# Moving the largest expert and the last pair of small ones in the order of 32 experts, with its row turning and one eviction placed elsewhere

## The chip, the core and the metric

One core of a Trainium2 chip runs the whole kernel. TensorE (PE in the profile) multiplies into PSUM; VectorE (DVE), ScalarE (ACT) and GpSimd (POOL) work beside it; SyncE (SP) issues the weight loads. All work in order, each on its own queue, and wait for one another by semaphores. The metric is the device time of one execution, in microseconds (us).

## The reference

A hybrid encoder layer on 512 tokens of width 1024: RMSNorm, one input projection into four head groups (stick-breaking attention, RG-LRU, HGRN2, Mamba-2), an output projection with a residual, and then a mixture of experts (MoE), which is where the change lies:

```python
logits = (xt @ router_w + router_b); top_logits, top_idx = lax.top_k(logits, 4)   # 32 experts
gates = softmax(top_logits)
# for each expert e, over the tokens routed to it:
hmid = xt[tok] @ w_gu[e] + b_gu[e]                  # 1024 -> 2048
glu = minimum(hmid[:, 0::2], 7); lin = clip(hmid[:, 1::2], -7, 7)
act = glu * sigmoid(1.702 * glu) * (lin + 1)
y = act @ w_down[e] + b_down[e]                     # 1024 -> 1024
# per token: the sum over its 4 experts of gate * y, added to h; a final RMSNorm
```

All of it is float32. Every expert has 12 MB of weights (8 MB for the first product, 4 MB for the second), and each is read once.

## The kernel before

The part ahead of the MoE is not touched. The router sorts the experts by their number of tokens, and the table CAPS gives each rank a capacity in rows: the largest 160, twelve others 120 to 72, sixteen 64, one 32, two 64. The experts are then worked one after another in an order written out by hand: the string SEQ (L55) names the kind of each place, and BIG says at which H, counted from 0, the largest expert stands. Rank r of a kind goes to the next place of that kind.

**Three kinds of expert.** H ("large", 65 to 128 rows) multiplies in a fast float32 mode that needs each operand in two parts, so each weight chunk is split on the fly: ACT copies it to the high part (L613) and DVE subtracts to get the low part (L614), in half chunks of 128x1024 through three buffers, so at most three half chunks ahead of PE. Three products of two matmuls each use one half chunk (L629). L ("small", 64 rows) and B (32 rows) multiply the chunk as it is, in plain float32, two (four) matmuls side by side in PE's columns (L658 and L729; L724 for B's second product). The largest expert is an H of 128 rows and a B of 32 rows in the same place; they share its weights.

**A stage.** The loop over the order (`for j, us in enumerate(seq)`) has one pass, here called stage j, per expert. In stage j, PE does: the bias of expert j (L644); its first product, in 8 steps k, one weight chunk each; then, while DVE and ACT do the activation of j (`act`, L674 to L679), the second product of expert j-1 in 8 steps f, two per chunk. At the end `yout(prev)` brings the result of j-1 out of PSUM with its gates (ACT L742 or L761, DVE L744 or L763), and `back` transposes the activation of j for its second product (L696; L687 for a B). So a stage that holds an H after an L is 8 chunks of fast product and 4 of plain product, and an L after an H the other way round.

**What is threaded between the steps.** `prepare` fetches the rows of a later expert: `onehot` (DVE L549), then `ids` (four small matmuls L556 into a PSUM bank, and the DVE reduction L557 that empties it) and a gather by POOL. `turn` transposes fetched rows into the layout for the first product (PE L585, then ACT L589 or L593, DVE L597 or L591). Rows are fetched and turned in groups: one per H, and one for up to 128 rows of L and B in a row. The dictionary `where` says in which stage a group is turned: "A" in the first product of an H, at k == 2; "B" at f == 5 of the second product of an H; "M" right after `act`. A "M" group of a stage with two units used the second half of the PSUM tile `hL` and one bank of the two-bank pool `m`. That tile's first half holds the first product of the B unit. `hot` (DVE L770) makes the matrix S which puts an expert's rows back to their tokens, and `add` (PE L789, DVE L791) adds all finished experts to the output in the stage after an H.

**Loads.** Weight chunks of 1 MB are loaded by SP in exactly the order of use, into a ring of 11 buffers: 8 chunks of expert j, then 4 of j-1's second product. A buffer is free when PE (for L, B) or the split on DVE (for H) has read it. The loads can so run less than one expert ahead of PE.

Stage numbers before, with the kinds: 0 L, 1 L, 2 H, 3 L, 4 H, 5 L, 6 L, 7 H+B (the largest), 8 L, 9 H, 10 L, 11 L, 12 H, 13 L, 14 H, 15 L, 16 L, 17 H, 18 L, 19 H, 20 L, 21 L, 22 H, 23 L, 24 H, 25 L, 26 H, 27 L, 28 H, 29 B, 30 H, 31 L. In stage 0, `run(first, ...)` threads the steps of the router's tables between the matmuls, one step after each k, and from k == 4 on one more in the middle.

Of the kernel before, what the change touches and what calls it, by code (L numbers as in the profile page):

```python
# [51 lines left out]

CAPS = (160, 120, 104, 104, 96, 96, 88, 80, 80, 72, 72, 72, 72) + 16 * (64,) + (32, 64, 64)

SEQ, BIG = "LL" + 4 * "HLHLL" + 3 * "HL" + "HBHL", 2  # L55
NSP = 3
FIN = "aaqqrAQrASQrAQrSSss"

# [420 lines left out]
def moe(ctx, tc, a, out, acc, c, loads, rt, mp, mp_es, hp, s2p, bp, early, once_es):  # L479
# [6 lines left out]
    def bank():  # L486
        return ps["m"].tile([128, 512], F32, name="m")
# [32 lines left out]
    N = len(seq)  # L520
# [125 lines left out]
    def gemm1(us, chunk, k, splits, limit, mid=lambda: None):  # L646

        W = chunk(k)
        last = k == KD - 1
        for u in us:  # L650
            if u.kind == "H":
                for half in range(2):
                    wh, wl = splits.take()
                    three(u.h[2 * half:2 * half + 2], u.xH[:, k, :], u.xL[:, k, :], wh, wl, False, last)
                    splits.make(limit)
            else:
                for q in range(4):
                    nc.tensor.matmul(u.h[q], u.xT[:, k, :], W[:, 512 * q:512 * q + 512], start=False, stop=last)  # L658
                    if q == 1:
                        mid()  # L660
# [20 lines left out]
    def back(us):  # L681

        for u in us:
            if u.kind == "B":
                p = u.views[0][1]
                for j in range(2):
                    nc.tensor.transpose(p[:, 128 * j:128 * j + 128], u.av[:, j:256:2], ident)  # L687
                u.aT = s2p.tile([128, 512], F32, tag="s2", name="aT")[:, 0:256].rearrange("p (j q n) -> p j q n", j=2, q=4)
                nc.scalar.activation(u.aT.rearrange("p j q n -> p (j q n)"), p[:, 0:256], AF.Copy)
                continue  # L690
            ps_ = [u.bk[0][:, 0:512], u.bk[1][:, 0:512]] if u.kind == "H" else [u.views[0][1][:, 0:512]]
            m = u.m
            for b, p in enumerate(ps_):
                for t_ in range(4):
                    f0 = 512 * b + 256 * (t_ // 2) + t_ % 2
                    nc.tensor.transpose(p[:, m * t_:m * t_ + m], u.av[0:m, f0:512 * b + 256 * (t_ // 2) + 256:2], ident[0:m, 0:m])  # L696
            if u.kind == "H":
                aH = wk.tile([128, KD, 128], FR, name="aH")
                aL = wk.tile([128, KD, 128], FR, name="aL")
                u.aH, u.aL = aH[:, :, 0:m], aL[:, :, 0:m]  # L700
                pv = [p[:, 0:4 * m].rearrange("p (k n) -> p k n", n=m) for p in ps_]
                for b in range(2):
                    nc.scalar.activation(u.aH[:, 4 * b:4 * b + 4, :], pv[b], AF.Copy)
                for b in range(2):
                    nc.vector.tensor_tensor(u.aL[:, 4 * b:4 * b + 4, :], pv[b], u.aH[:, 4 * b:4 * b + 4, :].bitcast(F32), op=OP.subtract)
            else:
                u.aT = wk.tile([128, 4, 2, 64], F32, name="aTL")
                nc.scalar.activation(u.aT.rearrange("p k g n -> p (k g n)"), ps_[0], AF.Copy)
# [56 lines left out]
    def hot(us):  # L765

        for u in us:
            if u.S is None:
                u.S = wk.tile([128, T], FR, name="S", bufs=3)[0:u.m]
                nc.vector.tensor_scalar(u.S, iota[0:u.m, :], u.tok[0:u.m, :], None, op0=OP.is_equal)  # L770
# [22 lines left out]
    splits = Splits([loads.of(j) for j, us in enumerate(seq) if us[0].kind == "H"])  # L793
# [3 lines left out]
    for g, us in enumerate(groups):  # L797
        j = us[0][0].j
# [21 lines left out]
    def turn_at(x, j, banks):  # L820
        for g in where.get((x, j), []):
            while g not in have:
                prepare()
            turn(g, *have[g], banks())
            turned.add(g)

    two = lambda: [bank(), bank()]
    halves2 = lambda: (lambda h: [h[:, 0:512], h[:, 512:1024]])(pair())
# [5 lines left out]
    def run(g, n=1000):  # L834
        for _ in range(n):
            if next(g, "end") == "end":
                return
# [5 lines left out]
    first = steps(rt.tables(), rt.more())  # L843
# [6 lines left out]
            ids(seq[e][0])  # L850
            yield

    pending = []
    for j, us in enumerate(seq):
        u = us[0]
        kind = u.kind
        if j == 1:
            once_es.close()
            sp = splits.pool = ctx.enter_context(tc.tile_pool(name="sp", bufs=NSP))
        if j == 2:  # L860
            mp_es.close()
            hL = ctx.enter_context(tc.tile_pool(name="hL", bufs=1, space=PSUM, side="right"))
            ps["m"] = ctx.enter_context(tc.tile_pool(name="m2", bufs=2, space=PSUM, side="right"))
        if j >= 1:
            loads.before(j + 1)

        if j == 0:
            u.views, u.h = [(0, rt.h0[0])], rt.h0[1]
        else:
            hL_ = [pair() if j < 2 else hL.tile([128, 1024], F32, name="hL")] if us[-1].kind != "H" else None  # L870
            light = lambda: hL_
            for x in us:
                if x.kind == "H":
                    x.bk = [pair(), pair()]
                bias(x, x.bk if x.kind == "H" else light() if x.kind == "L" else [light()[0][:, 0:512]])
        hi = heavy.index(j) if kind == "H" else 0
        after = heavy.index(j - 1) if j and seq[j - 1][0].kind == "H" else None
        for k in range(KD):
            if j == 0:
                gemm1(us, loads.of(j), k, splits, (hi, 16), lambda: run(first, k > 3))  # L880
                run(first, 1)
                continue
            gemm1(us, loads.of(j), k, splits, (hi, 16))
            if j == 1:
                if k == 0:
                    run(first)
                elif k < 5:
                    prepare()
                if k == 3:
                    back(seq[0])  # L890
                if k == 5:
                    mine = own()
                if k > 4:
                    run(mine, 2 if k == 7 else 1)
            elif k % 2:
                prepare()
            if kind == "H" and k == 2:
                turn_at("A", j, two)
            if kind != "H" and j > 1:
                if k == 3:  # L900
                    hot(pending)
                if after is not None and k > 4:
                    splits.make((after, 24), 1)
        act(us)
        if j == 0:
            continue
        if j > 1:
            turn_at("M", j, halves2 if kind != "H" and j > 1 else (lambda: [hL_[0][:, 512:1024], bank()]) if len(us) > 1 else two)

        prev = seq[j - 1]  # L910
        pk = prev[0].kind
        if pk == "H":
            hot(pending)
            limit = (after, 24) if kind != "H" and not (j + 1 < N and seq[j + 1][0].kind == "H") else (after + 1, 16)
            if len(prev) > 1:
                for i in range(NT):
                    add(pending, i)
        else:
            limit = None
        if j == 1:  # L920
            bd = rt.bdown()
        for f in range(KD):
            if pk == "H" and len(prev) == 1 and pending and 0 < f <= NT:
                add(pending, f - 1)
            gemm2(prev, loads.of(j - 1), f, splits, limit, u.views[0][1][:, 512:1024] if len(prev) > 1 else None)
            if j == 1:
                run(bd, 1)
                if f == 2:
                    turn_at("M", j, two)
                if f == 5:  # L930
                    back(us)
            elif pk != "H" and f in (2, 5):
                prepare()
            if pk == "H" and f == 4 and kind != "H":
                back(us)
            if f == 6 and len(us) > 1:
                back(us[1:])
            if pk == "H" and f == 5:
                turn_at("B", j, halves2)
            if pk != "H" and j + 1 < N and seq[j + 1][0].kind == "H" and f > 4:  # L940
                splits.make((heavy.index(j + 1), 16), 1)
        if pk == "H":
            pending = []
        pending = pending + prev
        yout(prev)
        if j > 1 and (pk != "H" or kind == "H"):
            back(us[:1])

# [62 lines left out]
    with tc.If(nblk > 0):  # L1011
        with tc.For_i(0, nblk, 1) as b, tc.manual_schedule():
# [11 lines left out]
            def chunk(q):  # L1024
                if q not in got:
                    got[q] = moe_chunk(nc, loads.slots, a, reg, q)
                return got[q]
# [999 lines left out]
```

## Time and profile before

| | us |
|---|---|
| median of 3 runs (1372.44 to 1380.81) | 1378.11 |
| the profiled execution | 1376.71 |
| its span, first to last instruction | 1374.9 |
| PE busy in it | 1312.0 (95%) |
| DVE busy | 882.4 (64%) |
| ACT busy | 643.6 (47%) |

The MoE's first stage begins 318.6 us into the span, its last at 1308.6. PE's busy time says little here, since matmuls overlap in it: two stages with the same matmuls can both be 100% busy and differ in length. So the stages are compared by their lengths, from the first bias matmul (L644) of one to that of the next.

### The profile page before, as it was taken

Reading aid. Unit: us, or ns where it says so; the run is one execution under the profiler, and the core shown is the slowest. Engines: PE = TensorE matmul, PEld = TensorE weight load, DVE = VectorE, ACT = ScalarE, POOL = GpSimd, SP = SyncE. Lnnn points to the kernel's source line nnn. Section 1 sums busy time; section 2 is a strip of 40 time slices with the busy share of each in tenths; the row PEclk is TensorE's granted clock in tenths of the full one; section 3 lists DMA queues with packets and bytes.
Section 4 is the critical chain, followed back from the end, with each engine's and each line's share of the span. In section 5 each row is a group of like instructions: output and inputs, shape, how many; then the busy total and the mean of one; then the engine's idle time right before and its main releaser. Section 6 shows DMA issues by size and latency. Waiting matters only on the chain.

```text
span 1374.9 us, 17788 instructions
## 1 busy us (share of the span) xinstructions
PE 1312.0 (95%) x6460; PEld 768.3 (56%) x6460; DVE 882.4 (64%) x1215; ACT 643.6 (47%) x886; POOL 94.4 (7%) x162
## 2 busy tenths in 40 slices
PE   7999998898999999999999999999999999999994
PEld 6877773574365554456545655546544555464651
DVE  5457867675576754457546765748545667686865
ACT  5366667652154533336234542526334445454632
POOL 0000123020110002000010000200010000000001
PEclk9999997899999999999999999999999999999998
DMA  6312012087899999888999999999999999999982
GB/s 196 116 61 92 1 70 88 1 325 306 338 398 405 420 419 397 339 363 310 404 366 419 419 394 420 409 419 405 419 400 419 419 393 420 418 417 399 419 359 78
DMA packets 80801, 442.09 MB, mean 322 GB/s; under 512 B 10972, under 2 KB 25380, under 8 KB 31684
## 3 DMA queue, kind: packets, MB, share of 16 engines
q1 hardware_dynamic: 76708, 427.66, 77.7%
q0 software_dynamic: 3856, 12.72, 2.7%
q8 instruction: 52, 0.85, 0.3%
q10 hardware_dynamic: 144, 0.52, 0.1%
q14 instruction: 41, 0.34, 0.1%
HBM read 436.68 MB, written 4.19 MB: 321 GB/s over the span
## 4 chain that ended last, share of the span: by engine, by line
PE 77%; DMA 7%; DVE 7%; ACT 5%; issue 3%; POOL 1%; DVEq 0%; SPq 0%; ACTq 0%; POOLq 0%
PE h L629 18%; PE hL L658 14%; PE m L629 10%; PE m L729 7%; PE m L1198 6%; PE h L789 6%; DMA wch<-in_moe_w_down_dram 4%; DMA wch<-in_moe_w_gu_dram 3%; PE h L658 2%; DVE w L614 1%; PE h L1823 1%; PE m L1823 1%; PE h L696 1%; PE m L1202 1%; PE h L585 1%
## 5 line engine op out<-in xcount | busy, mean ns | idle before, releaser
L614 DVE TENSOR_TENSOR w<-wch,w 128x1024 fp32r<-128x1024 f32 x312 | 378.8, 1224 | 153.8 <-ACT w L613 145.5
L613 ACT ACTIVATE w<-wch 128x1024 fp32r<-128x1024 f32 x312 | 328.4, 1061 | 273.4 <-DMA wch<-in_moe_w_down_dram 98.7
L629 PE MATMUL h<-w,xx 128*72 128x512 f32 (+6 forms) x1248 | 301.9, 399 | 4.9 <-DVE w L614 4.5
L629 PEld LDWEIGHTS h<-w,xx 128*72 128x72 f32 (+6 forms) x1248 | 195.6, 159 | 102.8 <-DVE w L614 7.2
L658 PE MATMUL hL<-wch,xp 128*64 128x512 f32 (+1 forms) x1152 | 239.1, 593 | 1.1 <-DMA wch<-in_moe_w_gu_dram 1.1
L658 PEld LDWEIGHTS hL<-wch,xp 128*64 128x64 f32 (+1 forms) x1152 | 74.8, 134 | 148.8 <-issue 141.2
L729 PE MATMUL m<-wch,aTL 128*64 128x512 f32 x544 | 124.3, 603 | 0.2 <-DVE tg L557 0.2
L629 PE MATMUL m<-w,aH 128*72 128x512 f32 (+6 forms) x416 | 116.5, 400 | 3.4 <-ACT w L613 2.1
L675 ACT ACTIVATE ag<-ag 128x512 f32<-128x512 f32 (+7 forms) x46 | 28.6, 622 | 167.9 <-DVE ag L674 167.8
L629 PEld LDWEIGHTS m<-w,aH 128*72 128x72 f32 (+6 forms) x416 | 62.9, 158 | 39.7 <-issue 7.4
L565 POOL CAST ix<-tg 64x1 int32<-64x1 f32 (+8 forms) x31 | 19.0, 611 | 848.3 <-DVE tg L557 839.7
L791 DVE TENSOR_TENSOR acc<-acc,h 128x1024 f32<-128x1024 f32 (+1 forms) x61 | 72.9, 1198 | 6.4 <-PE h L789 6.4
L729 PEld LDWEIGHTS m<-wch,aTL 128*64 128x64 f32 x544 | 37.0, 138 | 69.2 <-issue 67.2
L763 DVE SCALAR_TENSOR_TENSOR yS<-m,tg,yS 64x512 fp32r<-64x512 f32 (+1 forms) x38 | 28.5, 750 | 71.4 <-ACT yS L761 71.0
L1198 PE MATMUL m<-uH,wh 128*128 128x512 f32 x176 | 71.9, 408 | 0.8 <-DVE uL L1305 0.8
L1198 PE MATMUL m<-uH,wl 128*128 128x512 f32 x176 | 70.1, 398 | 0.5 <-DVE wl L1164 0.4
L1198 PE MATMUL m<-uL,wh 128*128 128x512 f32 x176 | 69.9, 397 | 0.0
L629 PE MATMUL m<-w,aL 128*72 128x512 f32 (+6 forms) x208 | 65.1, 394 | 0.0
L761 ACT ACTIVATE yS<-m,tg 64x512 fp32r<-64x512 f32 (+1 forms) x38 | 25.9, 681 | 74.9 <-PE m L729 72.4
L789 PE MATMUL h<-yS,S 128*128 128x512 f32 (+1 forms) x168 | 54.9, 400 | 2.4 <-DVE acc L791 1.3
L674 DVE TENSOR_SCALAR ag<-hL 128x512 f32<-128x512 f32 (+1 forms) x18 | 11.9, 659 | 64.5 <-PE hL L658 64.5
L1164 DVE TENSOR_TENSOR wl<-wnat,wh 128x1024 fp32r<-128x1024 f32 (+1 forms) x26 | 31.5, 1223 | 30.3 <-ACT wh L1163 30.3
(500 smaller groups left out, 1634.0 us busy)
## 6 DMA issues: line engine op xcount, KB each, us to landing
wch<-in_moe_w_gu_dram SPq DMA_DIRECT2D x256, 1024.0 KB
wch<-in_moe_w_down_dram SPq DMA_DIRECT2D x127, 1024.0 KB
wnat<-in_w_in_dram SPq DMA_DIRECT2D x12, 1024.0 KB
wch<-in_w_out_dram SPq DMA_DIRECT2D x4, 1024.0 KB
xin<-in_x_dram SPq DMA_DIRECT2D x4, 512.0 KB
acc<-in_x_dram SPq DMA_DIRECT2D x4, 512.0 KB
xdr<-wch POOLq DMA_DIRECT2D x4, 512.0 KB, 7.5
out_dram<-fo SPq DMA_DIRECT2D x3, 512.0 KB
```

The source lines that it names most:

```text
L613: nc.scalar.activation(wh, w, AF.Copy)
L614: nc.vector.tensor_tensor(wl, w, wh.bitcast(F32), op=OP.subtract)
L629: nc.tensor.matmul(ps_[q], x, w[:, 512 * q:512 * q + 512], start=start and z == 0, stop=stop and z == 2)
L658: nc.tensor.matmul(u.h[q], u.xT[:, k, :], W[:, 512 * q:512 * q + 512], start=False, stop=last)
L675: nc.scalar.activation(g, g, AF.Gelu_apprx_sigmoid)
L729: nc.tensor.matmul(u.y[0][64 * dh:64 * dh + 64, :], u.aT[:, 2 * (f // 4) + f % 2, (f // 2) % 2, :], W[:, 512 * dh:512 * dh + 512], start=f ...
L763: nc.vector.scalar_tensor_tensor(u.yS[o_, dh, :], y[s_, :], u.gate[s_, :], u.yS[s_, dh, :].bitcast(F32), op0=OP.mult, op1=OP.subtract)
L789: nc.tensor.matmul(hh[:, 512 * dh:512 * dh + 512], s, y, start=z == 0, stop=z == len(todo) - 1)
L791: nc.vector.tensor_tensor(o, o, hh[:, cols], op=OP.add)
L1164: nc.vector.tensor_tensor(wl, w, wh.bitcast(F32), op=OP.subtract)
L1198: nc.tensor.matmul(s.p, s.ws[q // 2][:, k, :], u_[:, k, :], start=(k == 0 and q == 0), stop=(k == KD - 1 and q == 2))
L1823: nc.tensor.matmul(p, m_(x, k)[:, 128 * i:128 * i + 128], ww, start=(k == 0 and q == 0), stop=(k == KD - 1 and q == 2))
```

## The change

The order becomes (places that differ: the largest expert goes from stage 7 to stage 12; of the four pairs "L L" between H's, the last goes from stages 20 and 21 to stages 26 and 27):

```
before  L L H L H L L H+B L H L L H   L H L L H L H L L H L H L H L H B H L
after   L L H L H L L H   L H L L H+B L H L L H L H L H L H L H L L H B H L
```

```diff
-SEQ, BIG = "LL" + 4 * "HLHLL" + 3 * "HL" + "HBHL", 2
+SEQ, BIG = "LL" + 3 * "HLHLL" + 4 * "HL" + "HLLHBHL", 4
...
-    pending = []
+    pending, late = [], []
...
             if j == 0:
-                gemm1(us, loads.of(j), k, splits, (hi, 16), lambda: run(first, k > 3))
+                gemm1(us, loads.of(j), k, splits, (hi, 16), lambda: run(first, k > 5))
...
             gemm1(us, loads.of(j), k, splits, (hi, 16))
+            if k == 1 and late:
+                yout(late)
+                late = []
...
-        if j > 1:
-            turn_at("M", j, halves2 if kind != "H" and j > 1 else (lambda: [hL_[0][:, 512:1024], bank()]) if len(us) > 1 else two)
+        if j > 1 and len(us) == 1:
+            turn_at("M", j, halves2 if kind != "H" else two)
...
+            if f == 4 and len(us) > 1:
+                turn_at("M", j, lambda: [hL_[0][:, 512:1024], bank()])
             if f == 6 and len(us) > 1:
                 back(us[1:])
+            if f == 6 and j == N - 1:
+                hot(prev + us)
...
-        yout(prev)
+        yout(prev[:1])
+        late = prev[1:]
```

In words: the eviction of the B unit of the largest expert moves from the end of the stage after it to the next stage, behind k == 1; a "M" group of the largest expert's stage would be turned at f == 4 and not right after `act`; the S matrices of the last two experts are made inside stage 31's second product and not behind it; and two steps of the router's tables leave the middle of k == 4 and k == 5 of stage 0.

How the instructions move, at three places. **PE, around the first product of the largest expert.** Its B unit's matmuls are the rows `hL<-wch,xp 32x512`; L585 are the transposes of fetched rows, L729 the second product of the L before it, L687 the B unit's activation. Before (stage 7):

```order
L629 MATMUL h<-w_4511,xx 128x512 x6
L629 MATMUL h<-w_4524,xx 128x512 x6
L658 MATMUL hL<-wch,xp 32x512 x4
L585 MATMUL hL<-ident,rows 128x128 x4
L585 MATMUL m<-ident,rows 128x128 x4
L729 MATMUL m<-wch,aTL 64x512 x6
```

Now (end of stage 11's first product, then the same place of stage 12):

```order
L658 MATMUL hL<-wch,xp 64x512 x32
L585 MATMUL h<-ident,rows 128x128 x16
L729 MATMUL m<-wch,aTL 64x512 x6
...
L629 MATMUL h<-w_5602,xx 128x512 x6
L629 MATMUL h<-w_5615,xx 128x512 x6
L658 MATMUL hL<-wch,xp 32x512 x4
L729 MATMUL m<-wch,aTL 64x512 x14
L687 MATMUL hL<-ident,avB 128x128 x2
```

The eight transposes into `hL` and `m` are gone from the largest expert's stage; sixteen stand one stage earlier, all into tile `h` (the H rows and, with them, one group of the B unit's and the next L's rows). No row is left for the new lines at f == 4.

**DVE, at the start of the second stage after the largest expert.** L614 are the splits of the weights, L763 the B unit's eviction, L744 the H unit's, L557 empties the bank of `ids`. Before (stage 9):

```order
L614 TENSOR_TENSOR w_4874<-wch,w_4874 128x1024
L763 SCALAR_TENSOR_TENSOR yS<-hL,tg,yS 32x512 x4
L744 SCALAR_TENSOR_TENSOR yL<-m,tg,yH 128x512 x2
L614 TENSOR_TENSOR w_4941<-wch,w_4941 128x1024
L614 TENSOR_TENSOR w_4950<-wch,w_4950 128x1024
L614 TENSOR_TENSOR w_4959<-wch,w_4959 128x1024
L614 TENSOR_TENSOR w_4968<-wch,w_4968 128x1024
L557 TENSOR_REDUCE tg<-m 96x2
```

Now (stage 14):

```order
L614 TENSOR_TENSOR w_5933<-wch,w_5933 128x1024
L744 SCALAR_TENSOR_TENSOR yL<-m,tg,yH 128x512 x2
L614 TENSOR_TENSOR w_5991<-wch,w_5991 128x1024
L614 TENSOR_TENSOR w_6000<-wch,w_6000 128x1024
L614 TENSOR_TENSOR w_6009<-wch,w_6009 128x1024
L614 TENSOR_TENSOR w_6018<-wch,w_6018 128x1024
L763 SCALAR_TENSOR_TENSOR yS<-hL,tg,yS 32x512 x4
L557 TENSOR_REDUCE tg<-m 88x2
L614 TENSOR_TENSOR w_6047<-wch,w_6047 128x1024
L614 TENSOR_TENSOR w_6056<-wch,w_6056 128x1024
L591 COPY xp<-m 128x512
```

The four evictions moved behind four splits, and stand now ahead of the reduction of `ids`. ACT's four (L761) moved in the same way.

**PE, in the same stage 14 now.** Between k == 1 and the end of k == 2:

```order
L629 MATMUL h<-w_5991,xx 96x512 x6
L556 LDWEIGHTS G
L556 MATMUL m<-mv,G 88x6
...
L629 MATMUL h<-w_6000,xx 96x512 x6
L629 MATMUL h<-w_6009,xx 96x512 x6
L585 MATMUL m<-ident,rows 128x128 x8
L629 MATMUL h<-w_6018,xx 96x512 x6
```

In the second stage after the largest expert there was no row L585 before; stage 14 has one, because its group is of kind "A". It takes both banks of the pool `m`, and the second of them is the bank that `ids` (L556) filled just before.

## Rows read from the trace of the kernel before

**Rows 1.** The page's chain of waits, by engine.

```profile
PE 77%; DMA 7%; DVE 7%; ACT 5%; issue 3%; POOL 1%; DVEq 0%; SPq 0%; ACTq 0%; POOLq 0%
```

**Rows 2.** Stretches: length, busy time by engine, granted clock, DMA share, GB/s.

```profile
534.10:583.20 49.10, 45.44 (x230) 24.25 (x230) 23.79 (x28) 19.04 (x23) 2.73 (x4) 0.97 0.90 349
622.00:659.30 37.30, 34.62 (x150) 21.61 (x148) 25.46 (x29) 19.93 (x24) 1.18 (x2) 0.91 0.84 315
717.50:748.60 31.10, 31.10 (x144) 19.05 (x141) 21.20 (x21) 17.59 (x20) 0.00 (x0) 1.00 1.01 419
748.60:782.70 34.10, 34.10 (x162) 19.63 (x162) 21.60 (x25) 13.49 (x17) 0.00 (x0) 1.00 1.01 420
782.70:815.60 32.90, 32.73 (x163) 20.12 (x161) 25.38 (x31) 18.81 (x21) 3.28 (x5) 1.00 1.02 393
815.60:847.20 31.60, 31.60 (x146) 17.32 (x146) 19.54 (x21) 10.84 (x14) 0.00 (x0) 1.00 1.01 419
847.20:870.20 23.00, 23.00 (x117) 8.17 (x117) 9.51 (x14) 5.84 (x9) 4.58 (x1) 1.00 1.01 420
782.70:902.60 119.90, 119.73 (x579) 65.06 (x577) 76.78 (x91) 53.62 (x62) 10.70 (x10) 1.00 1.01 409
902.60:937.80 35.20, 34.20 (x161) 19.09 (x161) 21.23 (x25) 13.23 (x17) 0.00 (x0) 1.00 1.01 419
968.90:1001.30 32.40, 32.40 (x154) 17.59 (x153) 19.91 (x22) 11.21 (x15) 0.00 (x0) 1.00 1.01 419
1056.60:1094.60 38.00, 34.62 (x161) 18.55 (x161) 21.13 (x25) 13.13 (x17) 0.00 (x0) 1.00 1.01 419
1094.60:1255.40 160.80, 160.80 (x761) 88.05 (x759) 115.69 (x128) 82.39 (x94) 6.83 (x9) 1.00 1.01 408
1255.40:1308.60 53.20, 53.08 (x291) 29.92 (x290) 43.43 (x47) 30.93 (x37) 0.00 (x0) 1.00 1.01 419
659.30:1308.60 649.30, 644.12 (x3091) 349.74 (x3090) 426.84 (x483) 294.70 (x343) 27.28 (x31) 1.00 1.01 410
```

**Rows 3.** Timeline: the activation of stage 7 and the transposes behind it.

```profile
570.43 0.42 DVE L677 TENSOR_SCALAR avB<-hL 128x256 f32<-128x256 f32 x1
570.91 0.66 PE L585 MATMUL hL<-ident,rows 128*128 128x128 f32 x4 [2.85 <-DVE avB L677]
```

**Rows 4.** Stretches behind PE's waits in stages 7 and 9, columns as in Rows 2.

```profile
571.60:575.00 3.40, 3.40 (x12) 1.22 (x12) 0.69 (x1) 0.60 (x1) 0.00 (x0) 0.50 0.16 67
629.60:636.40 6.80, 5.81 (x17) 4.08 (x18) 4.50 (x5) 1.83 (x2) 0.67 (x2) 0.50 0.68 252
```

**Rows 5.** Timeline: start of stage 9, the evictions and the wait.

```profile
624.93 3.03 DVE L763 SCALAR_TENSOR_TENSOR yS<-hL,tg,yS 32x512 fp32r<-32x512 f32 x4 [1.50 <-ACT yS L761]
630.59 2.04 PE L629 MATMUL h<-w,xx 128*104 128x512 f32 x4 [2.68 <-DVE w L614]
```

**Rows 6.** Timeline of stage 14: the bank of `ids`, then the "A" transposes.

```profile
791.46 0.15 DVE L557 TENSOR_REDUCE tg<-m 88x2 f32<-88x6 f32 x1
792.00 1.03 PE L585 MATMUL m<-ident,rows 128*128 128x128 f32 x8
```

**Rows 7.** PE's waits in stage 23: us in total, times, longest.

```profile
PE m L629 <- ACT w L613: 1.7, 1, 1.7
PE hL L658 <- DMA wch<-in_moe_w_gu_dram: 1.1, 2, 0.6
```

**Rows 8.** Timeline of stage 0: the wait at the router's tables.

```profile
342.08 0.32 PE L419 MATMUL m<-sc,early 32*96 32x1 f32 x2 [0.96 <-DVE sc L417]
```

**Rows 9.** Timeline of stage 31: first split of the second product, last S matrices.

```profile
1320.89 2.00 ACT L613 ACTIVATE w<-wch 128x1024 fp32r<-128x1024 f32 x2 [9.74 <-DMA wch<-in_moe_w_down_dram]
1322.92 1.15 PE L629 MATMUL m<-w,aH 128*72 128x512 f32 x4
1341.36 1.41 DVE L744 SCALAR_TENSOR_TENSOR yL<-m,tg,yH 72x512 fp32r<-72x512 f32 x2 [2.83 <-ACT yH L742]
1343.31 0.47 PE L789 MATMUL h<-yH,S 72*128 72x512 f32 x1 [1.45 <-DVE S L770]
```

## The prediction

> **What bounds the kernel now.** I read the chain of waits first, by engine [rows 1]: PE holds 77% of the span and loads 7%, so the chain runs through PE's own work, with loads in a few places. Then I cut the MoE into its stages [rows 2]. From stage 10 to stage 30 loads run at 410 GB/s, and the DMA share is full. An expert is 12 chunks of 1.049 MB, so 12.58 MB / 410 GB/s = 30.7 us per stage is what the loads need. PE needs, in stages that wait for nothing: 31.1 us for an H after an L (32.9 with an "A" turn in it), 31.6 for an L after an H (32.4 with a "B" turn of an L group, 34.1 with that and a third finished expert to add, which is so behind a pair), 23.0 for the second L of a pair. Thus PE sets the pace nearly everywhere by one or two us per stage, and the second L of a pair takes 30.7 - 23.0 = 7.7 us from the lead of the loads. The reader should see four stages that are longer than their kind: 7 (49.1, the largest expert), 9 (37.3 against 31.1), 18 (35.2 against 34.1) and 23 (38.0 against 34.1). The change touches all four.
>
> The sum is made on the profiled execution (1376.7 us); the median of the runs shown is 1.4 higher.
>
> **Turning the rows: -4.5.** In stage 7 PE's transposes write into the second half of `hL` and wait 2.85 us until DVE has read the B unit's product out of that tile [rows 3]. Right behind this wait PE's granted clock is 0.50 for 3.4 us, 1.2 instead of 2.4 GHz [rows 4], which loses 1.7. The order shows that the transposes do not move to f == 4, as the new lines would have it, but out of the stage: with the largest expert at stage 12 its B unit and the L behind it are one group, turned in stage 11 into tile `h`. So the new lines at f == 4 have nothing to do, and the wait goes all the same: behind the first product PE finds stage 11's second product, which is ready. The transposes cost PE the same one stage earlier (16 in a row, and the plain second product behind them covers their copies on ACT and DVE): 0. 2.8 + 1.7 = 4.5; at least 2.8, if the clock falls somewhere else instead.
>
> **The B unit's eviction: -3.8.** In stage 9 DVE runs the four evictions (3.03 us) and the H unit's two ahead of the fourth half chunk's split, and PE waits 2.68 us for it [rows 5]; then the clock is at half for 6.8 us [rows 4], 3.4 lost. 2.7 + 3.4 = 6.1, and the stage is 6.2 over its kind [rows 2]; I take 6.0. Without the four, that split comes 3.03 earlier, and the wait is gone. They are late next in stage 14: ACT's four lie behind the seventh half chunk's split, DVE's too, and behind DVE's four now stands the reduction that frees the bank of `ids`. PE wants this bank for the second four of the eight "A" transposes. In stage 14 before, the reduction ended at 791.6 and PE came to the second four at about 792.5 [rows 6]: 0.9 of room. With 3.03 more on DVE PE waits 2.2 (estimate). The splits queued behind are two half chunks away from PE, and with PE waiting they catch up. -6.0 + 2.2 = -3.8. Ends: -6.0 without a wait; -0.4 if the clock then falls as long as in stage 9. Waits of 2.68 and 2.85 were followed by half clock, one of 1.7 in stage 23 was not (its stage shows 1.00) [rows 2, 7]; 2.2 lies between, and I take no fall.
>
> **The order and the loads: -5.0 +1.0 +0.2.** Stages 18 and 23 lose 1.1 and 3.9 us over the 34.1 of stage 13, in 23 visibly to loads [rows 2, 7]. I keep a book of the spare, by how much a chunk lands before an L stage behind an H needs it; each stage adds its length less 30.7. At 18 it is zero. Between the ends of 13 and 17 lie 119.9 us [rows 2], 4 x 30.7 = 122.8, so at 13 it was 2.9. In the new order stages 13 to 18 repeat the old 8 to 13 kind by kind, with the ring full behind the largest expert, so stage 18 has these 2.9 and doesn't wait: both waits go. Seven stages of H and L follow without a pair; five such last 160.8 [rows 2], 32.2 each, so +1.5 each: 2.9 + 10.5 = 13.4 at stage 26. Stage 26 (31.6) +0.9, stage 27 -7.7, stage 28 +1.5: 8.1 at stage 29. Stages 29 and 30 were 53.2 [rows 2], now 1.7 more for a third expert to add (34.1 - 32.4): 54.9 - 61.4 = -6.5, so 1.6 at stage 31, no wait. As a check, the old order: zero at 23, +7.3 for 24 to 28, -8.2 for 29 and 30, -0.9 at 31, where the trace has the first split of the second product begin on a landing at 1320.89 and PE start at 1322.92, 1.0 of it the conversion on ACT: 1.0 spare [rows 9]. The book is good to 2 us. It holds if the ring, 11 chunks or 28 us less what is in use, can keep 13 ahead; seen so far are 7.3 with the rate not falling. With 7.3 as the limit stage 31 would wait 5.3. I take 1.0, nearer to zero, since 408 GB/s over those five stages show no sign of a limit; ends 0 and 5.3. Stage 8 is now an L behind a pair without a refill before it, between stage 13 (0) and 18 (1.1); I take 0.2, end 3.9.
>
> By the Trainium skill ("DMA: Bandwidth & Descriptors", Specifications) the fabric's ceiling is 435 GB/s; at that an expert would be an estimated 28.9 us, loads would never be late in the new order, and these terms would be -5.0 alone. The rows have 410 in the mean and 420 at most, and the sum goes by 410.
>
> **Small terms.** Stage 0: PE waits 0.96 for the router's tables [rows 8]; with the step moved one k later, all matmuls of a further chunk stand in between: -1.0 (at worst 0). Stage 31: the last S matrices are ready before, and PE then waits for the first half of the 1.41 us of L744 instead of 1.45 for S [rows 9]: -1.2 (ends -1.4 and -0.2). Two L groups go from "B" turns or the old "M" to "A": by kind 1.8 against 0.8 [rows 2], +1.2 for both (0 to +2.0).
>
> Sum: -4.5 - 3.8 - 5.0 + 1.0 + 0.2 - 1.0 - 1.2 + 1.2 = **-13.1**. 1376.7 - 13.1 = 1363.6, and 1.4 more against the median: **1365 us**. What a measurement of this kernel can tell from no change is about 1%, 13.8 us, so the lines are 1364.3 and 1391.9: the forecast lies just inside.
>
> **Rivals.** (A) No new wait in stage 14, no wait at the end: -6.0 for the eviction and 0 for the end, -16.3, **1362**, and 1360 with the other small ends. For it: the split lead of three half chunks, which I may underrate. (B) The pair near the end drains the ring: limit 7.3, 5.3 instead of 1.0, and one fall of the clock (3.4) behind it: -13.1 + 4.3 = -8.8, **1369**, or 1373. For it: only four stages follow the pair, two of them (29, 30) below 30.7. (C) The wait in stage 14 halves the clock for 6.8 us as in stage 9: -9.7, **1368**. (D) Slower: the largest expert's long stages refilled the ring at stage 7 (349 GB/s there, 315 in stage 9, ring full) [rows 2]; now they come five stages and one pair later. Stages 7 to 11 would last 31.1 + 34.1 + 32.9 + 31.6 + 23.0 = 152.7 against 153.5, even at 30.7 per expert. At 393 GB/s, the rate in stage 14, an expert is 32.0 and they lose 7.3; the rivals' other losses on top (B's 4.3 + 3.4) would about undo the gain. The order is slower than before from 13.1 / 5 = 2.6 us more per expert on (378 GB/s), which no undisturbed stage shows; at 370 (34.0) it gives **1382**. The Trainium skill ("DMA: Bandwidth & Descriptors", Where 436 GB/s comes from) lets HBM bind such loads at about 358 GB/s; that would be an estimated 35.1 us per expert and a kernel paced by loads in any order, and the rows disagree with 410 to 420.
>
> **How the numbers follow.** Forecast 0.43, A 0.22, B 0.18, C 0.12, D 0.05. Faster by over 1%: A but for 0.01, and 0.17 of the forecast, whose centre is 0.7 above the line with about 4 us of doubt either way: 0.38. Slower by over 1% is only the far end of D, beyond 1391.9: 0.03. Within 1%: 0.59. The range leaves out D, the far end of A and of B: the low end is A with its small ends less 2 for the scatter of the runs (they spread from 1372 to 1381), 1358; the high end B with the clock fall and 2: 1375.
>
> **What would show it.** Right: stage 12 about 43 us long (49.1 - 4.5 - 1.3 for the transposes) with no wait behind its first product and the clock at 1.00; in stage 14 no wait for the fourth half chunk, a wait of some 2 us at L585 for DVE's L557; stages 18 to 28 without waits on loads; at 29 to 31 at most 1 us of them; no wait at L419 and less than 0.5 at the first L789 of stage 31. Wrong: PE waiting for `w` or `wch` in stages 8, 29 or 31, or a clock of 0.50 in the MoE behind a wait that I have at 2 us.

## The result, and the profile after

The changed kernel takes **1365.64 us** (median of 4 runs, 1364.77 to 1366.82); the kernel before, run beside it, 1377.42 (4 runs, 1372.44 to 1380.81). The ratio is 0.992, with a 95% interval from 0.9892 to 0.9947: 11.8 us faster by the medians, 0.8% by the ratio (0.5 to 1.1% by its interval). The forecast was 1365 (1358 to 1375), "within 1%" at 0.59. The number held; two of its terms did not, and other small differences made up for them, which is luck. In the profiled executions the span fell by 10.4, from 1374.9 to 1364.5, where the sum had 13.1.

The chain of waits by engine, which answers to [rows 1]: loads go from 7% to 3%, PE from 77% to 82%.

```profile
PE 82%; DVE 7%; ACT 6%; DMA 3%; issue 2%; POOL 1%; DVEq 0%; ACTq 0%; POOLq 0%
```

The stages of the kernel after that answer to [rows 2 and 4]: 12 (the largest expert), 14 (the eviction's new place), half clock in 14, 18, 29, half clock in 29, and the eleven stages from 18 to 28 as one. Columns: length, busy time of PE, PE's weight loads, DVE, ACT and POOL, granted clock, DMA share, GB/s.

```profile
685.50:728.30 42.80, 42.25 (x220) 22.81 (x217) 22.98 (x27) 18.36 (x22) 2.37 (x4) 1.00 1.00 402
767.20:805.00 37.80, 34.59 (x166) 21.11 (x164) 27.39 (x33) 20.52 (x25) 4.85 (x5) 0.95 0.88 318
781.00:784.40 3.40, 3.40 (x10) 2.21 (x9) 2.88 (x4) 1.06 (x1) 2.77 (x2) 0.50 0.40 101
894.00:927.80 33.80, 33.80 (x161) 19.12 (x161) 21.38 (x25) 13.32 (x17) 0.00 (x0) 1.00 1.01 420
1239.60:1271.90 32.30, 28.67 (x160) 16.60 (x160) 20.47 (x25) 12.80 (x17) 0.00 (x0) 0.95 1.01 420
1252.00:1255.50 3.50, 3.50 (x10) 2.68 (x9) 2.80 (x5) 1.87 (x3) 0.00 (x0) 0.51 1.01 419
894.00:1239.60 345.60, 345.51 (x1637) 186.08 (x1636) 233.00 (x262) 161.96 (x188) 13.33 (x17) 1.00 1.01 410
```

What to see: the largest expert's stage is 42.8 at full clock, and stage 18 is 33.8, where it was 35.2. Two stages are longer than their kind, that is, than undisturbed stages with the same work: 14 with 37.8 against 32.9, and 29 with 32.3, where 26.5 would be its kind (24.8, as pair_22 below shows it, and an estimated 1.7 for a third expert to add, the 34.1 - 32.4 of [rows 2]). In both the clock is at half behind a wait.

Timeline of PE, then DVE, then ACT in stage 14, which answers to [rows 6]. The number in brackets is the idle time before the row, and what ended it.

```profile
776.52 0.60 PE L585 MATMUL m<-ident,rows 128*128 128x128 f32 x4
780.16 0.66 PE L585 MATMUL m<-ident,rows 128*128 128x128 f32 x4 [3.04 <-ACT xp L593]
...
777.49 3.04 DVE L763 SCALAR_TENSOR_TENSOR yS<-hL,tg,yS 32x512 fp32r<-32x512 f32 x4 [1.43 <-ACT yS L761]
780.56 0.16 DVE L557 TENSOR_REDUCE tg<-m 88x2 f32<-88x6 f32 x1
...
774.71 2.74 ACT L761 ACTIVATE yS<-hL,tg 32x512 fp32r<-32x512 f32 x4
777.48 2.00 ACT L613 ACTIVATE w<-wch 128x1024 fp32r<-128x1024 f32 x2
779.51 0.60 ACT L593 ACTIVATE xp<-m 128x512 f32<-128x512 f32 x1
```

PE does four of the eight "A" transposes and waits 3.04 us for the second four. It goes on at 780.16, 0.05 behind the end of ACT's L593 (779.51 + 0.60) and 0.40 ahead of DVE's reduction L557. So it waited for the copy of the first four, and not for the bank of `ids`. The second four did not take the bank that `ids` had filled, as both the section on the change and the prediction had it. L593 stands on ACT behind the four evictions and two splits.

Timeline of PE and ACT in stage 29, a place that the prediction had nearly free of waits.

```profile
1246.50 1.06 PE L658 MATMUL hL<-wch,xp 128*32 128x512 f32 x8 [0.47 <-DMA wch<-in_moe_w_gu_dram]
1250.14 0.67 PE L629 MATMUL m<-w,aH 128*72 128x512 f32 x2 [2.57 <-ACT w L613]
1251.40 0.69 PE L629 MATMUL m<-w,aH 128*72 128x512 f32 x2 [0.59 <-DVE w L614]
...
1249.03 2.01 ACT L613 ACTIVATE w<-wch 128x1024 fp32r<-128x1024 f32 x2 [8.28 <-DMA wch<-in_moe_w_down_dram]
```

PE waits for ACT's split, and ACT, idle for 8.28, begins it when the chunk lands. PE's three waits are 3.6 us, all behind loads, and half of 3.5 is lost to the clock.

### The profile page after: what moved, and what is told of

Same layout as the page of the kernel before. It is cut to its first block, busy times and chain, and to the rows that moved or that the text cites. A ratio compares the mean times of both kernels' runs of the same rounds, so it can differ in the third digit from the quotient of the medians.

```text
span 1364.5 us, 17788 instructions
## 1 busy us (share of the span) xinstructions
PE 1308.4 (96%) x6460; PEld 767.3 (56%) x6460; DVE 883.0 (65%) x1215; ACT 644.3 (47%) x886; POOL 96.5 (7%) x162
## 4 chain that ended last, share of the span: by engine, by line
PE 82%; DVE 7%; ACT 6%; DMA 3%; issue 2%; POOL 1%; DVEq 0%; ACTq 0%; POOLq 0%
PE h L629 19%; PE hL L658 16%; PE m L629 11%; PE m L729 8%; PE m L1206 6%; PE h L789 6%; DMA wch<-in_moe_w_down_dram 2%; PE h L658 2%; DVE w L614 1%; PE h L1831 1%; PE h L696 1%; PE m L1831 1%; ACT w L613 1%; PE m L1210 1%; PE h L644 1%
## 5 line engine op out<-in xcount | busy, mean ns | idle before, releaser
L614 DVE TENSOR_TENSOR w<-wch,w 128x1024 fp32r<-128x1024 f32 x312 | 378.9, 1224 | 132.4 <-ACT w L613 124.7
L658 PE MATMUL hL<-wch,xp 128*64 128x512 f32 (+1 forms) x1152 | 238.4, 593 | 0.5 <-DMA wch<-in_moe_w_gu_dram 0.5
L658 PEld LDWEIGHTS hL<-wch,xp 128*64 128x64 f32 (+1 forms) x1152 | 75.0, 134 | 149.0 <-issue 143.0
L729 PE MATMUL m<-wch,aTL 128*64 128x512 f32 x544 | 122.7, 597 | 0.2 <-DVE tg L557 0.2
L763 DVE SCALAR_TENSOR_TENSOR yS<-m,tg,yS 64x512 fp32r<-64x512 f32 (+1 forms) x38 | 28.5, 750 | 74.3 <-ACT yS L761 74.0
L729 PEld LDWEIGHTS m<-wch,aTL 128*64 128x64 f32 x544 | 36.7, 136 | 69.2 <-issue 66.3
L761 ACT ACTIVATE yS<-m,tg 64x512 fp32r<-64x512 f32 (+1 forms) x38 | 25.9, 682 | 78.1 <-PE m L729 75.6
```

The lines of the kernel that those rows point to most:

```text
L614: nc.vector.tensor_tensor(wl, w, wh.bitcast(F32), op=OP.subtract)
L729: nc.tensor.matmul(u.y[0][64 * dh:64 * dh + 64, :], u.aT[:, 2 * (f // 4) + f % 2, (f // 2) % 2, :], W[:, 512 * dh:512 * dh + 512], start=f ...
L763: nc.vector.scalar_tensor_tensor(u.yS[o_, dh, :], y[s_, :], u.gate[s_, :], u.yS[s_, dh, :].bitcast(F32), op0=OP.mult, op1=OP.subtract)
```

## The experiments

All were timed beside the kernel before. Its medians in the three groups of runs were 1377.8, 1375.05 and 1376.68, so ratios are compared across groups and medians only within one.

**order_only.** The kernel before with the new first line alone (the order and the largest expert's place), none of the other edits.

> The new order and the new place of the largest expert alone; eviction, the steps of stage 0 and the S matrices of stage 31 as before. Theory (every part is worth what its own stage shows): the kernel after is 1365.6; the eviction then stands at the end of stage 13 again and PE waits for a split in stage 14 as it did in stage 9 (2.7 and half clock behind it), stage 14 about 39 us (37.8 after); the wait of 0.96 at the router's tables is back in stage 0 and 1.45 for S in stage 31. Together +1.3 +1.0 +1.6 = 1369.5, up to 1 more if the clock falls in stage 0. Stage 12 stays at 42.8, stage 29 at 32.2. Rival 1 (the order does it all, the other edits are hidden): 1366, within 0.5 of after. Rival 2 (the edits do most of it, the order gives back at the end what it takes): 1374 or more.

Measured: 1371.04, ratio 0.9963 (0.9939 to 0.9987). Stage 14 as a stretch, columns as above:

```profile
769.70:808.70 39.00, 36.14 (x164) 21.80 (x160) 27.27 (x34) 20.36 (x25) 3.12 (x5) 0.91 0.84 306
```

and PE's timeline in it:

```profile
778.32 2.02 PE L629 MATMUL h<-w,xx 128*96 128x512 f32 x4 [2.69 <-DVE w L614]
785.14 1.04 PE L585 MATMUL m<-ident,rows 128*128 128x128 f32 x8
```

The wait for the split is the one of [rows 5], now in stage 14, and the eight transposes stand together without a wait. The wait at the router's tables (1.0) and the one for S (1.5) are back too. By the interval rival 1 falls; rival 2 (1374 or more) lies partly inside it, up to 0.9987, and falls by the stages: every stage that the theory names came as it had it, and stage 29 is 31.6. The order is worth 5 to 7 us (5.1 by the ratio, 5.8 by the spans of the profiled executions, 6.8 by the medians), the other edits the rest. Moving the eviction is a small part of these: 39.0 against 37.8.

**late_f3.** The changed kernel, with the eviction moved again:

```diff
-            if k == 1 and late:
-                yout(late)
-                late = []
...
             elif pk != "H" and f in (2, 5):
                 prepare()
+            if f == 3 and late:
+                yout(late)
+                late = []
```

> The kernel after, with the B unit's eviction not behind k == 1 of stage 14's first product but at f == 3 of its second product, where ACT and DVE make no splits. Theory: the 3.04 us of PE's wait at the second four transposes, and the half clock behind it (3.4 us, 1.7 lost), come from ACT's and DVE's evictions standing ahead of the copies that empty the transposes' banks; without them stage 14 is 33.3 (its kind is 32.9) against 37.8, no clock of 0.50 near 781, 1365.6 - 4.5 = 1361.1. Rival 1 (loads pace what follows, so that time won here is waited for in stages 18 or 29): stage 14 33.3, but those stages longer by as much, 1365.6. Rival 2 (the transposes wait in any case, since the bank is late whatever stands ahead): stage 14 stays at 36 or more, 1364 to 1366.

Measured: 1360.26, ratio 0.9886 (0.9863 to 0.9909). Stage 14 as a stretch:

```profile
765.90:798.80 32.90, 32.73 (x164) 20.17 (x160) 27.40 (x34) 20.45 (x25) 3.27 (x5) 1.00 0.96 361
```

and the timeline of PE at its transposes and of DVE's evictions, now in the second product:

```profile
775.24 1.03 PE L585 MATMUL m<-ident,rows 128*128 128x128 f32 x8
...
794.82 3.03 DVE L763 SCALAR_TENSOR_TENSOR yS<-hL,tg,yS 32x512 fp32r<-32x512 f32 x4 [0.95 <-ACT yS L761]
```

The stage is at its kind, to a tenth; the wait and the fall of the clock are gone, and stage 18 is 33.9 long as in the kernel after, so nothing comes back behind it. Stage 29 keeps its wait of 2.57. The theory holds.

**late_k3.** The same three lines behind the "A" transposes of the first product, with `k == 3`.

> The kernel after with the B unit's eviction behind k == 3 of stage 14's first product: behind the A transposes, but still between splits. Theory (what costs in the kernel after is that PE waits for a bank at the transposes; the splits, three half chunks ahead, can nearly stand the evictions): ACT's 2.74 and DVE's 3.03 one behind the other hold up the splits by 4.2 to 4.5, against a lead of 3 x 1.37 = 4.1, so PE waits 0 to 1 for a split, stage 14 is 33 to 34, no clock of 0.50: 1361 to 1362. Rival (eight evictions cost PE 3 to 5 us wherever they stand between splits, and only the second product has room): stage 14 36 to 38, 1364 to 1366.

Measured: 1368.19, ratio 0.9943 (0.9925 to 0.9961); the kernel after in the same group 1366.97. Stage 14, and the stretch behind the wait in it:

```profile
768.80:808.00 39.20, 35.91 (x164) 21.73 (x160) 27.63 (x34) 20.25 (x25) 2.79 (x5) 0.91 0.85 301
789.70:796.50 6.80, 6.38 (x22) 4.11 (x23) 4.39 (x7) 2.11 (x2) 1.20 (x3) 0.50 0.79 304
```

The timeline of PE, then DVE, at the wait:

```profile
786.88 0.71 PE L629 MATMUL h<-w,xx 128*96 128x512 f32 x2 [0.76 <-ACT w L613]
790.12 2.02 PE L629 MATMUL h<-w,xx 128*96 128x512 f32 x4 [2.54 <-DVE w L614]
...
784.27 1.29 DVE L549 TENSOR_TENSOR G<-posP,iota 128x512 bf16<-128x512 f32 x2
785.78 3.03 DVE L763 SCALAR_TENSOR_TENSOR yS<-hL,tg,yS 32x512 fp32r<-32x512 f32 x4 [0.22 <-ACT yS L761]
788.84 3.49 DVE L614 TENSOR_TENSOR w<-wch,w 128x1024 fp32r<-128x1024 f32 x3
```

My expectation was wrong and the rival right in kind, though its price was too low (39.2 where it had 36 to 38): no transposes wait, and the stage is longer still. DVE makes no split from 784.27 to 788.84, 4.6 us (the one-hot of the next rows, which I had left out, stands in it too), and the lead of the splits is less than I took. That one of the three buffers is always with the matmuls that run would explain this; no run varies the number of buffers. Between splits the eight evictions cost PE 5 to 6 us in every place that was tried.

**big_old.** The changed kernel with `BIG` 2: the largest expert back at stage 7, where the new lines at f == 4 have rows to turn.

> The kernel after with the largest expert back at stage 7 (the pair stays at 26 and 27): now the rows that are turned in its stage are turned at f == 4, by the new lines. Theory: the wait of 2.85 for the activation's read is gone all the same, stage 7 is about 44.5; the eviction behind k == 1 of stage 9 has no transposes behind it and costs PE at most 1, stage 9 is 31 to 32; stages 7 to 16 together 326 against 330 in the kernel after. But the ring is then filled five stages earlier: stage 18 waits some 1.1 again, and the chunks of stage 29 land some 3 later, so that it is 35 long: 1365.6 - 4 + 1 + 3 = 1365 to 1366. Rival 1 (the place of the largest expert gives the loads nothing): stages 18 and 29 as in the kernel after, 1361 to 1362. Rival 2 (transposes at f == 4 wait for a bank or for POOL's rows): stage 7 is 47 or more, 1368 or more.

Measured: 1369.98, ratio 0.997 (0.9952 to 0.9989). Stages 7, 9, 18 and 29:

```profile
531.30:576.00 44.70, 43.89 (x230) 23.70 (x230) 23.32 (x27) 19.04 (x23) 2.47 (x4) 1.00 0.97 377
614.80:651.50 36.70, 33.44 (x148) 20.79 (x144) 25.71 (x29) 19.77 (x24) 2.93 (x2) 0.95 0.85 314
895.10:930.00 34.90, 34.23 (x161) 19.10 (x161) 21.19 (x25) 13.30 (x17) 0.00 (x0) 1.00 1.01 419
1241.80:1275.70 33.90, 29.63 (x160) 16.71 (x160) 20.48 (x25) 12.80 (x17) 0.00 (x0) 0.90 1.01 420
```

PE's timeline at the transposes of stage 7, then at the wait in stage 9:

```profile
569.63 0.66 PE L585 MATMUL hL<-ident,rows 128*128 128x128 f32 x4
570.12 0.60 PE L585 MATMUL m<-ident,rows 128*128 128x128 f32 x4
...
629.70 10.54 PE L629 MATMUL h<-w,xx 128*104 128x512 f32 x38 [2.72 <-DVE w L614]
```

Stage 7 came as expected: turned at f == 4, the rows cost no wait, 44.7 against 49.1. Stage 9 did not: with no transposes in the way PE waits 2.72 for a split, as long as in [rows 5], and the stage is 36.7 against 37.3. At its old place the eviction's move alone is thus worth 0.6. Stage 18 is 1.1 longer again, stage 29 1.6 longer. The total is 4 to 5 above what I expected, and that is stage 9.

**pair_22 and pair_20.** The changed kernel with the last pair at stages 22 and 23, or at its old place, 20 and 21:

```diff
-SEQ, BIG = "LL" + 3 * "HLHLL" + 4 * "HL" + "HLLHBHL", 4
+SEQ, BIG = "LL" + 3 * "HLHLL" + "HLHL" + "HLL" + "HLHL" + "HBHL", 4      # pair_22
+SEQ, BIG = "LL" + 4 * "HLHLL" + 3 * "HL" + "HBHL", 4                     # pair_20
```

> The kernel after, with the last pair of small experts at stages 22 and 23 and not 26 and 27. Theory: the 5.2 us too many of stage 29 come from the pair standing two experts ahead of a B stage, whose first product is shorter, so that the next chunks are needed earlier. At 22 the loads have regained their lead by stage 29: stage 29 about 25.5, no half clock in it, and the stage behind the pair (25) has some 2 us to spare: 1365.6 - 5.2 = 1360.4. Rival 1 (a pair drains the loads wherever it stands behind the largest expert): stage 25 waits 4 to 5 us, 1365. Rival 2 (the B stage itself is what the loads cannot feed, with the pair or without): stage 29 keeps its wait, 1365.6.

> The kernel after, with the last pair at stages 20 and 21, where it stood before the change; the largest expert stays at stage 12. It tells the two moves of the order apart. Theory (the later largest expert alone refills the ring late enough): the chunks of the stage behind the pair (23) land 5 to 6 us ahead of their use, against 1.9 before the change, so it waits 0 to 0.5 instead of 3.9, stage 18 has no wait, stage 29 has none: 1360.4 to 1361. Rival (it is the pair's move that took the waits away): stage 23 is 37 to 38 long again, 1364 to 1366.

Measured: 1363.05, ratio 0.9905 (0.9884 to 0.9926), and 1362.29, ratio 0.9901 (0.9881 to 0.9922). pair_22, stage 29, then stage 25 behind the pair:

```profile
1243.70:1268.50 24.80, 24.80 (x152) 14.13 (x152) 20.43 (x25) 12.72 (x17) 0.00 (x0) 1.00 1.01 421
1113.70:1147.60 33.90, 33.90 (x162) 18.54 (x162) 21.18 (x25) 13.17 (x17) 0.00 (x0) 1.00 1.01 420
```

pair_20, stage 23 behind the pair, then stage 29:

```profile
1044.90:1079.30 34.40, 34.13 (x161) 18.81 (x161) 21.12 (x25) 13.19 (x17) 0.00 (x0) 1.00 1.01 418
1240.10:1265.20 25.10, 25.10 (x152) 13.99 (x152) 20.20 (x25) 12.70 (x17) 0.00 (x0) 1.00 1.01 419
```

Both theories hold by stage. With the pair away from the end stage 29 waits for nothing; the stage behind the pair is 34.4 even at the old place, where it was 38.0 [rows 2]. So it is the largest expert's later place that took the waits of stages 18 and 23 away; the pair's own move cost 3.6 us of waits and a fall of the clock, and gave 0.5. By ratio the two stand 0.0015 and 0.0019 below the 0.992 of the kernel after and 0.0036 and 0.0040 below the 0.9941 of its second group (after_again), 2 to 5.5 us, where I had about 5. The intervals reach some 3 us to either side, so here the stages decide and not the medians: from the start of stage 1 to that of stage 31 the kernel after takes 951.4, each of these two 946.

**after_again, best22, best24, best20.** The kernel after once more, and late_f3's edit together with the pair at 22, at 24 (`"HLHLHL" + "HLL" + "HL" + "HBHL"` behind the three `HLHLL`) and at 20.

> The changed kernel itself, unaltered, beside the next three, so that they can be compared with it on the same chip: 1365.6 as before, 1364 to 1367; stage 14 at 37.8 and stage 29 at 32.2 again.

> Both mends together: the B unit's eviction at f == 3 of stage 14's second product, and the last pair at stages 22 and 23. Theory (two separate losses, neither a floor set by the loads): stage 14 32.9, stage 29 24.8, no wait behind the pair; from stage 1 to stage 31 the kernel after takes 951.4, the two alone took 945.4 and 945.9, so together 951.4 - 6.0 - 5.5 = 939.9 to 941 (1.1 of the 6.0 lay in stage 29 and can't be won twice), and the median 1365.6 - 10.4 = 1355, up to 1358 by the medians of the two alone. Rival (the time PE lost in stage 14 let the loads run ahead, and is paid at the pair): stage 25 or 29 waits 3 to 5 us, 1360.

> Both mends, with the last pair at stages 24 and 25, so between 22 (no wait seen) and 26 (3.6 us of waits and a fall of the clock in stage 29). A blind test of the book on the loads, kept now with the pace of the weights' own queue, 31.3 us per expert, and with the B stage's first product 6.9 us shorter than an L's (7.0 against 13.9). Theory: in best22 the last chunk of stage 27's first product landed 11.1 ahead of its use, in pair_20 the one of stage 23 behind the pair 4.4; here stage 27 stands behind the pair, with 7 or so, no wait; by stage 29 two stages of about 1 us each and one of 2.7 more have been won, 2 less than in best22, so stage 29 waits 0 to 1.5 for its chunks, not long enough for a fall of the clock: stage 29 is 25 to 26.5 long, the median within 1.5 of best22's 1356.9, 1356 to 1359. Rival 1 (the ring limits the lead, or any pair ahead of the B stage within five stages dries it): stage 29 at 29 to 31 with the clock at 0.50 behind the wait, 1361. Rival 2 (stage 27 waits instead, as stage 23 did in the kernel before): 1360.

> Both mends, with the last pair where it stood before the change, stages 20 and 21; only the largest expert's place in the order differs from the kernel before. Theory: as pair_20 (stage 23 34.4 with 0.5 of waits, stage 29 25.0) with stage 14 at 32.9: 1362.3 - 4.9 = 1357.4, within 1.5 of best22. Rival (a shorter stage 14 leaves the loads less time ahead of the pair): stage 23 waits 3 or more again, 1360 to 1361.

Measured: after_again 1366.97, ratio 0.9941 (0.9922 to 0.9959); best22, in the same group, **1356.87**, 0.9875 (0.9844 to 0.9907); in another group, best24 1358.69, 0.9867 (0.9838 to 0.9895), and best20 1358.46, 0.986 (0.9834 to 0.9886). best22, stages 14, 25 and 29:

```profile
765.60:798.60 33.00, 32.83 (x166) 20.20 (x164) 27.44 (x34) 20.55 (x25) 3.27 (x5) 1.00 0.96 363
1105.30:1139.20 33.90, 33.90 (x162) 18.54 (x162) 21.14 (x25) 13.20 (x17) 0.00 (x0) 1.00 1.01 419
1235.30:1260.10 24.80, 24.80 (x152) 14.13 (x152) 20.48 (x25) 12.77 (x17) 0.00 (x0) 1.00 1.01 419
```

best24, stage 29 as a stretch:

```profile
1238.30:1264.30 26.00, 25.12 (x151) 13.92 (x151) 20.14 (x25) 12.63 (x17) 0.00 (x0) 1.00 1.01 419
```

and PE's timeline in it, from the B unit's first product:

```profile
1238.49 7.04 PE L658 MATMUL hL<-wch,xp 128*32 128x512 f32 x64
1245.84 0.69 PE L629 MATMUL m<-w,aH 128*72 128x512 f32 x2 [0.30 <-ACT w L613]
1247.10 0.68 PE L629 MATMUL m<-w,aH 128*72 128x512 f32 x2 [0.57 <-DVE w L614]
```

The two mends add up: best22 is 10.1 below the kernel after on the same chip, and beats both kernels. best24's stage 29 is 26.0 with the clock at 1.00, as the mended book on the loads had it. Between these three places of the pair (20, 22 and 24) the runs show no difference beyond 2 us.

## Why the prediction was right, and where it was not

**Turning the rows, -4.5: right.** Stage 12 is 42.8 where 43 was forecast, at full clock. 49.1 - 42.8, less the 1.3 of transposes that went to stage 11, is 5.0. big_old adds that f == 4 would have done as well.

**The eviction, -3.8: wrong size, and the wrong bank.** Measured is -1.3: stage 9 was 6.2 over its kind, stage 14 is 4.9 over. The step put 3.03 more us on DVE and let PE wait 2.2 for L557. What it left out stood in [rows 5]: DVE's four begin 1.50 late, because ACT's four come first, and ACT's 2.74 hold up ACT's own splits and copies as well. PE waited 3.04 for L593, and the clock fell for 3.4 us, which the step took as not falling; rival C had the fall, at 6.8. late_f3 shows that no cost is left when both engines are free, late_k3 and big_old that a place between splits costs 5 to 6. So the step that failed is the wait: it was put on one engine and one bank, and the evictions hold up two engines.

**The order and the loads, -5.0: right, and by the largest expert alone** (pair_20). In the row of stages 18 to 28 above PE is busy for 345.51 of 345.60 us. The spare of 2.9 at stage 18, on which the step rested, came right by luck, as shown below.

**The end, +1.0: wrong; it was +5.3** (0.47 + 2.57 + 0.59 of waits and 1.7 of clock). Two steps of the book failed (the prediction's running account of the spare, by how much a chunk lands before it is needed). The first is the pace. 30.7 us per expert was worked out from 410 GB/s, which holds all that the DMA engines moved, the gathered rows among it. The queue of the weights by itself (packets, MB, share), of the kernel after from 894.0 to 1239.6:

```profile
q1 hardware_dynamic: 19031, 138.60, 98.4%
```

138.60 MB / 345.6 us = 401 GB/s, so 31.4 us per expert. Eleven of them are 345.4, and PE took 345.6: from stage 18 to 29 the spare stayed at 2.9 + 0.2 = 3.1 where the book had 8.1. The kernel before would have told it: its row from 902.6 to 1255.4,

```profile
q1 hardware_dynamic: 19519, 142.16, 98.8%
```

gives 403 GB/s and 31.2. The second is the B stage: its first product is 7.0 us long (best24's row of L658), an L's 13.9, so the chunks behind it are wanted 6.9 earlier. 3.1 - 6.9 = -3.8, and 3.6 were measured. Neither step alone would have made PE wait: 8.1 - 6.9 = 1.2 with the book's pace, 3.1 with a first product as long as an L's.

The check on the old order, 1.9 off, did not show the pace, and the landings show why. The first split of a second product on ACT begins when its chunk lands. In the kernel after in stage 18, with PE's first use of it:

```profile
904.06 2.01 ACT L613 ACTIVATE w<-wch 128x1024 fp32r<-128x1024 f32 x2 [8.89 <-DMA wch<-in_moe_w_down_dram]
908.25 1.15 PE L629 MATMUL m<-w,aH 128*88 128x512 f32 x4
```

and in the kernel before in stages 18 and 23:

```profile
916.27 2.01 ACT L613 ACTIVATE w<-wch 128x1024 fp32r<-128x1024 f32 x2 [12.47 <-DMA wch<-in_moe_w_down_dram]
1073.12 2.01 ACT L613 ACTIVATE w<-wch 128x1024 fp32r<-128x1024 f32 x2 [15.36 <-DMA wch<-in_moe_w_down_dram]
```

From 904.06 to 1249.03 (stage 29) eleven experts land, 31.4 us each; before, from 916.27 to 1073.12 five, 31.4 each, and from there to 1320.89 (stage 31 [rows 9]) eight, 31.0 each. The book counted one stage too few between such places: four from 13 to 18, seven from 23 to 31, ten from 18 to 29. The stage left out was longer than its load, which hid a pace that was too fast. From 13 to 18 five stages last 34.1 + 119.9 = 154.0 [rows 2] and their loads 5 x 31.4 = 157.0: 3.0, where four stages at 30.7 gave 2.9. In the trace the spare at 18 is 3.1 (908.25 less the end of the first split, 904.06 + 1.06). In the check the part left out, from PE's start behind the wait of stage 23 (1074.22) to the end of that stage and from the start of stage 31 to PE's first use of such a split (1322.92 [rows 9]), lasts 34.7, some 3.5 over a load. From 18 to 29 the same slip worked the other way: with stage 18 counted the book would have had 3.1 more still.

Rival B had the loads behind the pair late and about this price, but at stage 31 and for another reason: no limit of the ring is seen, since the DMA share is 1.01 in the row of stages 18 to 28. The Trainium skill's ceiling ("DMA: Bandwidth & Descriptors", Specifications) of 435 GB/s would by estimate have made these waits 0. The weights' own 401 GB/s speak against planning with it.

**Small terms.** Stage 0: the wait of 0.96 at L419 is gone; the stage is 2.0 shorter, and the other 1.0 goes with a fall of the clock near 322 us that this execution did not have. The MoE began 1.0 earlier, by a part that the change doesn't touch. Stage 31: the wait of 1.45 for S is gone, 1.6 in all (1.2 forecast). Stage 8: 34.5, +0.4 (0.2 forecast). The +1.2 for two more "A" turns was not measured by itself; the turns are there (stages 9, 14, 17, 21, 25 and 28, where before it were 14, 17, 24 and 28).

The two wrong terms were 2.5 and 4.3 too good, 6.8 together. Turning (0.5), stages 0 and 31 and the start (2.4) and tenths in many stages gave some 4 back in the profiled execution, the spread of the runs the rest. That the time came out within 1 us is thus luck, the turn of the rows and the waits of stages 18 and 23 are not. Both signs that the prediction named as "wrong" appeared: PE waiting for `w` in stage 29, and a clock of 0.50 behind the wait in stage 14.

## What to carry to other kernels

- An edit that moves work off one queue is priced on every queue that it runs through: here two engines work one behind the other, and the second starts when the first has ended. Look for a place where both have nothing to feed, and not for a later place among the same splits.
- A book on loads is kept with the pace of their own queue, and with the moment at which each stage wants its first chunk; a short stage behind a run of full ones wants it early. Count as many loads as land between the two moments.
- A number that comes out right can rest on two wrong terms: compare stage by stage before believing the sum.

## What the runs showed that I had not expected

- The second four transposes waited for the copy of the first four. In order_only, late_f3 and late_k3 the same eight stand together without a wait. What makes the pool give another bank was not tried by itself.
- PE waits of 2.44 to 3.04 us in the MoE were followed by a granted clock of 0.50 (1.2 GHz) for 3.4 to 6.8 us: late_k3 2.44 and 2.54, after 2.57 and 3.04, order_only 2.69, big_old 2.72. In this kernel such a wait cost some 1.7 to 3.2 more than it lasted, half of the time that PE worked at 0.50. The 6.8 stands where the clock fell while PE still waited (late_k3: at 789.7, and PE went on at 790.12), the 3.4 where it fell behind the wait (after: at 781.0, and PE had gone on at 780.16).
- Behind the waits of 0.30 and 0.57 in best24 the clock stayed at 1.00. But in order_only it also fell for 3.4 us at 381.8, in stage 2, where no wait just before it is longer than 0.53: a long wait is not the only thing that a fall follows.
